# The first branch projection of a gated two-branch decoder block, computed in seven block products per pair of feature units (Strassen's scheme, one level)

## The chip, the cores and the metric

The kernel runs on one NeuronCore of a Trainium2 chip. The metric is device time in microseconds (us) for one launch. The kernel before was timed three times: 597.3, 597.81 and 597.81 us, median 597.81 us. One more execution was recorded by the profiler, and every duration in this text comes from that one.

The engines are named as in the profile: PE is TensorE (matmuls), PEld its weight loads, DVE is VectorE, ACT is ScalarE, POOL is GpSimd, SP is the queue that issues DMAs.

## The reference, cut to what matters

One decoder layer on 512 tokens and 16 meta tokens, width 1024, in float32. Two attention branches are computed from the same normed input `u`, each is gated, projected back to the model width, and the two are merged:

```python
u = rmsnorm(h, pre_norm_g)
proj = u @ w_in                       # all branch inputs and gates
...
o_mla = causal_block_attention(q_m, k_m, v_mla, MLA_SCALE)
y_mla = (o_mla * silu(z_mla)) @ w_br_mla            # 1024 x 1024, the second branch here (br 0)
...
o_fox = causal_block_attention(fq, fk, fv, FOX_SCALE, cum)
y_fox = (o_fox * silu(z_fox)) @ w_br_fox            # 1024 x 1024, the first branch here (br 1)
mixed = (sigmoid(gate_a) * y_mla + sigmoid(gate_b) * y_fox) @ w_out
h = h + rmsnorm(mixed, post_norm_g)
return h[:, N_META:]
```

The change is in the line for `y_fox` and in the order of the gate projections (`gate_a`, `gate_b`) around it.

## The kernel before

Every large matrix product is done in three passes. A float32 operand is split into a high part in the matmul type `fp32r` (an ACT copy) and the rest as a low part (a DVE or POOL subtraction), and the product is high x high + high x low + low x high. A weight that arrives by DMA as `wraw` (128 x 1024, 512 KB) so becomes `wh` and `wl`; the pool `wp` has three buffers of each of the three kinds, and a load waits until the buffer's earlier weight has been split.

Features lie on the partitions, in 8 blocks of 128 (`KD` = 8, `HK` = 4), tokens lie along the free dimension (`S` = 512). A "unit" (`unit`) is one output block of 128 features: 8 blocks of the contraction x 3 passes = 24 matmuls with a 128 x 128 weight held and 128 x 512 activations streamed, summed in one PSUM bank. A gate unit (`gate_unit`, tile `pg`) projects `u` and ends in a tanh on ACT into a tile `th` that a later step reads. A branch unit (`py`) projects the branch output `gT[br]` (split into `gh`, `gl` by `halved_g`) and ends in one DVE instruction, (th + 1) * PSUM, back into `gT[br]`.

The program has three stages: the input norm and small projections, sixteen attention stages (8 pairs of heads x 2 branches) with projections filled in between, and the merge stage. The change is in the merge stage. On PE the program order is kept as it is written (`manual_schedule`); ACT and DVE are ordered by a scheduler, each engine runs its own list in order, and SP issues the DMAs in its own order.

The merge stage before: `halved_g(1)` splits the first branch's output; then eight units `py(i, 1)`, with a gate unit after each of the first three; then `halved_g(0)` and four gate units; then eight units `py(i, 0)` of the second branch with the last four gate units between, and the sums for the output projection (`ssum`). The output projection itself is already done in seven block products on quarter matrices; the differences of its weight blocks (`tb`, loaded by eight DMAs in the merge stage) are formed by `tsum` on DVE.

The tanh results live in a pool `thp` of five buffers.

Of the kernel before, what the change touches and what calls it, by code (L numbers as in the profile page):

```python
# [11 lines left out]
F32 = mybir.dt.float32  # L12
F32R = mybir.dt.float32r
# [4 lines left out]
ALU = mybir.AluOpType  # L18
AX = mybir.AxisListType
PSUM = bass.MemoryType.PSUM  # L20
# [3 lines left out]
S = 512  # L24
META = 16
L = S + META
NH = 16
KD = D // 128
# [21 lines left out]
def f32(ap):  # L50
    return ap.bitcast(F32)
# [3 lines left out]
def block_kernel(ctx: ExitStack, tc: tile.TileContext, x, meta_tokens, pre_norm_g, w_in, fox_forget_b,  # L55
                 mla_q_norm_g, mla_kv_norm_g, w_uq, w_ukv, w_br_mla, w_br_fox, w_out, post_norm_g,
                 rope_tok, rope_pe, out):
    nc = tc.nc
# [4 lines left out]
    wbr = [w_br_mla[0].rearrange("(k p) f -> p k f", p=128), w_br_fox[0].rearrange("(k p) f -> p k f", p=128)]  # L63
# [19 lines left out]
    wp = ctx.enter_context(tc.tile_pool(name="wp", bufs=3))  # L83
    uid = [0]
# [3 lines left out]
    def dma(out, src, start=None):  # L88

        with tc.issue_after(sums_out[0]) if written[0] and sums_out else nullcontext():  # L90
            ins = (start or nc.sync.dma_start)(out=out, in_=src)
        if written[0]:
            tc.keep_in_program_order(ins)
        return ins.ins

    def mm(*a, **k):
        nc.tensor.matmul(*a, **k)  # L97
# [4 lines left out]
    def split_lo(eng, lo, src, hi):  # L102
        return eng.tensor_tensor(out=lo, in0=src, in1=f32(hi), op=ALU.subtract)  # L103
# [30 lines left out]
    def wunit(srcs):  # L134
        return wsplit(wload(srcs))
# [27 lines left out]
    thp = ctx.enter_context(tc.tile_pool(name="thp", bufs=5, side="right"))  # L163
# [9 lines left out]
    ths = {}  # L173
# [83 lines left out]
    with ExitStack() as ph:  # L257
# [262 lines left out]

    gctx = ctx.enter_context(ExitStack())
    PAIRED = [i + 4 * j for i in range(4) for j in range(2)]
    gates = [(i, 1) for i in range(KD)] + [(i, 0) for i in PAIRED]

    def gate_unit():

        i, br = gates.pop(0)

        def done(_, ps):
            ths[i, br] = thp.tile([128, L], F32, tag="th", name=f"th{i}{br}")[:, 0:S]  # L530
            nc.scalar.activation(ths[i, br], ps, AF.Tanh, scale=0.5)
        return unit(f"pg{i}{br}", win_w((O_GA, O_GB)[br], i), u_act, KD, REAL, done)


    with ExitStack() as att:
# [25 lines left out]
        gT = []  # L561
        masks, normed = [], []
# [361 lines left out]
        for si, (br, pr) in enumerate(stages):  # L924
            last = si + 1 == len(stages)
# [65 lines left out]
    with ExitStack() as mg:  # L991
        mg.enter_context(tc.manual_schedule(engines={mybir.EngineType.PE}))
        m1 = mg.enter_context(tc.tile_pool(name="m1", bufs=1, side="right"))
        mgg = ExitStack()
        m2 = mgg.enter_context(tc.tile_pool(name="m2", bufs=1))
        HK = KD // 2
        gh, gl = (m2.tile([128, KD, S], F32R, tag=n, name=n) for n in ("gh", "gl"))
        tb = [m1.tile([128, HK, 512], F32, tag=f"tb{n}", name=f"tb{n}") for n in range(4)]
        a1 = [m1.tile([128, HK, 256], F32R, tag=n, name=n) for n in ("a1h", "a1l")]
        a2 = [m1.tile([128, HK, S], F32R, tag=n, name=n) for n in ("a2h", "a2l")]  # L1000
        mx = gT[0]
        sh, sl = ([t.rearrange("p k s -> p (k s)")[:, 1024 * j : 1024 * j + 1024].rearrange("p (k s) -> p k s", k=HK)
                   for j in range(4)] for t in uT0)

        def halved_g(br):
            for k in range(KD):
                nc.scalar.copy(gh[:, k], gT[br][:, k])
                split_lo(nc.vector, gl[:, k], gT[br][:, k], gh[:, k])

        def py(i, br):  # L1010
            def get():
                return by_k(wunit([wbr[br][:, :, 128 * i : 128 * i + 128]])[0], KD)

            def done(_, ps):
                nc.vector.scalar_tensor_tensor(out=gT[br][:, i], in0=ths[i, br], scalar=1.0, in1=ps, op0=ALU.add, op1=ALU.mult)
            run(unit(f"py{i}{br}", get, lambda k: (gh[:, k, :], gl[:, k, :]), KD, [slice(0, S)], done))
            if br:
                return
            nc.vector.tensor_tensor(out=mx[:, i], in0=mx[:, i], in1=gT[1][:, i], op=ALU.add)
            src, (h, l) = (mx[:, i, 0:256], [t[:, i] for t in a1]) if i < HK else (mx[:, i], [t[:, i - HK] for t in a2])  # L1020
            nc.scalar.copy(h, src)
            split_lo(nc.vector, l, src, h)

        def tsum(n, half):

            ks = slice(2 * half, 2 * half + 2)
            t11, t12, t22, t21 = (t[:, ks] for t in tb)
            out, a, b = ((t11, t12, t11), (t12, t22, t12), (t22, t22, t11), (t21, t21, t22))[n]
            nc.vector.tensor_tensor(out=out, in0=a, in1=b, op=ALU.subtract)
# [9 lines left out]
                nc.scalar.copy(h[:, ks], x)  # L1039
                split_lo(nc.vector, l[:, ks], x, h[:, ks])  # L1040

        halved_g(1)
        for i in range(KD):
            py(i, 1)
            if i < 3:
                run(gate_unit())
            if i == 2:
                for n, (kb, c) in enumerate(((0, 0), (0, 1), (1, 1), (1, 0))):
                    for half in range(2):
                        k0 = HK * kb + 2 * half  # L1050
                        nc.sync.dma_start(tb[n][:, 2 * half : 2 * half + 2], wout[:, k0 : k0 + 2, 512 * c : 512 * c + 512])
            if i >= 4:
                for half in range(2):
                    tsum(i - 4, half)
# [72 lines left out]
        X, Z = ([op5.tile([128, 512], F32, tag="po", name=f"{n}{r}") for r in range(2)] for n in "xz")  # L1127
        Y = [acc(f"y{r}") for r in range(2)]
# [86 lines left out]
```

## Time and profile before

| | us |
|---|---|
| three timed runs | 597.3, 597.81, 597.81 |
| the profiled execution, time | 597.2 |
| the profiled execution, span from first to last instruction | 595.1 |
| PE busy | 586.8 (99%) |
| DVE busy | 379.2 (64%) |
| ACT busy | 343.1 (58%) |
| POOL busy | 201.6 (34%) |

The span is what the profile divides up; 2.1 us of the profiled execution's time lie outside it. A busy PE only says that some matmul was in flight: matmuls overlap, so a matmul's own duration is longer than the distance from its start to the next one's. What a row of matmuls costs is read from the chain of waits, which gives the stretch of time for a number of matmuls in a row. The mean granted TensorE clock was 0.997 of full.

### The profile page before, as it was taken

Reading aid. Unit: us, or ns where it says so; the run is one execution under the profiler, and the core shown is the slowest. Engines: PE = TensorE matmul, PEld = TensorE weight load, DVE = VectorE, ACT = ScalarE, POOL = GpSimd, SP = SyncE. Lnnn points to the kernel's source line nnn. Section 1 sums busy time; section 2 is a strip of 40 time slices with the busy share of each in tenths; the row PEclk is TensorE's granted clock in tenths of the full one; section 3 lists DMA queues with packets and bytes.
Section 4 is the critical chain, followed back from the end, with each engine's and each line's share of the span. In section 5 each row is a group of like instructions: output and inputs, shape, how many; then the busy total and the mean of one; then the engine's idle time right before and its main releaser. Section 6 shows DMA issues by size and latency. Waiting matters only on the chain.

```text
span 595.1 us, 10741 instructions
## 1 busy us (share of the span) xinstructions
PE 586.8 (99%) x3697; PEld 496.8 (83%) x3697; DVE 379.2 (64%) x1096; ACT 343.1 (58%) x785; POOL 201.6 (34%) x271
## 2 busy tenths in 40 slices
PE   8999999999999999999999999999999999999996
PEld 6989889889888888898898898878888888888884
DVE  5845876775776766757748747854634524377957
ACT  7846775784765765757748747942223422353753
POOL 4417656364458463544544554420000000000000
PEclk9999999999999999999999999999999999999998
DMA  8535699998995998896987887868533332333503
GB/s 298 118 82 172 124 165 269 217 206 202 181 198 125 208 225 219 187 184 166 201 166 175 190 171 149 193 165 305 155 85 92 106 107 73 105 106 104 215 2 141
DMA packets 219998, 97.45 MB, mean 164 GB/s; under 512 B 131456, under 2 KB 209672, under 8 KB 219944
## 3 DMA queue, kind: packets, MB, share of 16 engines
q1 hardware_dynamic: 219944, 96.77, 68.6%
q8 instruction: 29, 0.48, 0.3%
q14 instruction: 25, 0.20, 0.1%
HBM read 62.36 MB, written 3.97 MB: 111 GB/s over the span
## 4 chain that ended last, share of the span: by engine, by line
PE 98%; DMA 1%; SPq 0%; DVE 0%; issue 0%; POOL 0%; DVEq 0%; ACT 0%; POOLq 0%
PE z L97 17%; PE pg L97 15%; PE py L97 15%; PE v L97 9%; PE st L97 8%; PE fk L97 8%; PE fq L97 8%; PE ov L97 5%; PE psm L97 4%; PE x L97 4%; PE mq L97 2%; PE mk L97 1%; PE ppe L97 1%; PE y L97 1%; DMA wsr<-in_w_in_dram 1%; PE pt L100 1%
## 5 line engine op out<-in xcount | busy, mean ns | idle before, releaser
L103 POOL TENSOR_TENSOR wl<-wraw,wh 128x1024 fp32r<-128x1024 f32 (+2 forms) x62 | 119.6, 1936 | 92.5 <-ACT wh L130 70.1
L130 ACT CAST wh<-wraw 128x1024 fp32r<-128x1024 f32 (+1 forms) x80 | 83.1, 1042 | 116.0 <-PE pg L97 38.5
L787 ACT ACTIVATE sf<-sf,nb 128x272 f32<-128x272 f32 (+3 forms) x128 | 72.5, 568 | 16.8 <-DVE nb L779 15.3
L815 DVE SCALAR_TENSOR_TENSOR pn<-sf,ri,pn 128x128 f16<-128x128 f32 (+3 forms) x128 | 68.6, 576 | 6.6 <-ACT pn L814 6.2
L103 DVE TENSOR_TENSOR wl<-wraw,wh 128x1024 fp32r<-128x1024 f32 x34 | 41.5, 1222 | 42.1 <-ACT wh L130 42.0
L814 ACT ACTIVATE pn<-sf,ri 128x128 f16<-128x128 f32 (+3 forms) x128 | 61.2, 549 | 9.3 <-ACT sf L787 7.4
L97 PE MATMUL z<-uTh,wh 128*128 128x512 f32 x128 | 51.0, 398 | 0.0
L97 PE MATMUL pg<-uTh,wh 128*128 128x512 f32 x128 | 50.3, 393 | 0.0
L97 PE MATMUL z<-uTl,wh 128*128 128x512 f32 x128 | 50.2, 392 | 0.0
L97 PE MATMUL z<-uTh,wl 128*128 128x512 f32 x128 | 50.0, 390 | 0.0
L97 PE MATMUL pg<-uTh,wl 128*128 128x512 f32 x128 | 49.9, 389 | 0.0
L97 PE MATMUL pg<-uTl,wh 128*128 128x512 f32 x128 | 49.8, 389 | 0.0
L97 PE MATMUL py<-gh,wh 128*128 128x512 f32 x128 | 49.8, 389 | 0.0
L97 PE MATMUL py<-gl,wh 128*128 128x512 f32 x128 | 49.8, 389 | 0.0
L97 PE MATMUL py<-gh,wl 128*128 128x512 f32 x128 | 49.8, 389 | 0.0
L97 PE MATMUL st<-hlk,hlq 64*128 64x272 f32 (+3 forms) x480 | 45.5, 308 | 0.0
L97 PEld LDWEIGHTS st<-hlk,hlq 64*128 64x128 f32 x480 | 34.6, 185 | 6.0 <-ACT vh L702 2.8
L683 DVE TENSOR_REDUCE vsc<-v 128x1 f32<-128x272 f32 (+1 forms) x32 | 13.2, 432 | 39.9 <-PE v L97 39.9
L97 PE MATMUL v<-uTh,wl 128*128 128x256 f32 (+1 forms) x128 | 36.5, 285 | 0.0
L97 PE MATMUL fk<-uTl,wh 128*128 128x256 f32 (+1 forms) x128 | 36.5, 285 | 0.0
L97 PE MATMUL fk<-uTh,wh 128*128 128x256 f32 (+1 forms) x128 | 36.4, 285 | 0.0
L97 PE MATMUL v<-uTl,wh 128*128 128x256 f32 (+1 forms) x128 | 36.4, 285 | 0.0
(234 smaller groups left out, 1458.8 us busy)
## 6 DMA issues: line engine op xcount, KB each, us to landing
wraw<-in_w_in_dram SPq DMA_DIRECT2D x56, 512.0 KB, 4.6
cbp<-c_dram SPq DMA_DIRECT2D x16, 264.0 KB, 4.5
wraw<-in_w_br_fox_dram SPq DMA_DIRECT2D x8, 512.0 KB, 8.1
tb<-in_w_out_dram SPq DMA_DIRECT2D x8, 512.0 KB, 4.7
wraw<-in_w_br_mla_dram SPq DMA_DIRECT2D x8, 512.0 KB, 3.5
wraw<-in_w_out_dram SPq DMA_DIRECT2D x6, 512.0 KB, 3.7
xr<-in_x_dram SPq DMA_DIRECT2D x4, 512.0 KB
out_dram<-yo SPq DMA_DIRECT2D x8, 256.0 KB, 2.0
```

Of the source, the lines that this page charges most:

```text
L97: nc.tensor.matmul(*a, **k)
L100: nc.tensor.transpose(*a)
L103: return eng.tensor_tensor(out=lo, in0=src, in1=f32(hi), op=ALU.subtract)
L130: nc.scalar.copy(wh[:, :n], raw[:, :n])
L683: nc.vector.tensor_reduce(out=sc[:, i : i + 1], in_=ps, op=ALU.max, axis=AX.X, apply_absolute_value=True)
L787: exps[g] = nc.scalar.activation(sf, sf, AF.Exp, bias=sums["nb"][:, h, b : b + 1], scale=-1.0, accum_out=sums["su"][:, h, b : b + 1]).ins
L814: normed[:] = [nc.scalar.activation(hi, sf, AF.Copy, scale=rib).ins]
L815: nc.vector.scalar_tensor_tensor(out=lo, in0=sf, scalar=rib, in1=hi, op0=ALU.mult, op1=ALU.subtract)
```

## The change

The first branch's projection treats a pair of units (i, i + 4) at once. The weight's and the activations' halves (contraction blocks 0-3 and 4-7, tokens 0-255 and 256-511) make 2 x 2 block matrices, and the four output quarters come out of seven block products instead of eight. Each product is 4 contraction blocks x 3 passes = 12 matmuls with a 128 x 128 weight held and 128 x 256 activations streamed. The sums and differences that the scheme needs are formed on DVE: four of the activations once for all pairs, four of the weights in each pair. Every block that enters a product is split into a high and a low part (ACT copy, DVE subtraction): seven of the activations (128 x 1024 each) once, seven of the weights (128 x 512 each) in each pair.

Three PSUM banks a pair, X, Y and Z, hold the products. X runs through five of them: it is read by an ACT copy after the first and the third, by a DVE addition after the fifth, and at the end by the gating; each of the later products is added on top, so PE has to wait for that read before it starts the next product in X. The order on PE in a pair is X (A11), Z (S1), X (S2), Y (A12), X (S3), Z (S4), X (A22).

Two gate units run ahead of the first pair and two after each pair; one is left for the second branch's units. The gates are taken in the order 0, 4, 1, 5, ... for both branches, and two more tanh buffers (`thx`) are added.

```diff
-    gates = [(i, 1) for i in range(KD)] + [(i, 0) for i in PAIRED]
+    gates = [(i, br) for br in (1, 0) for i in PAIRED]
...
+        A11, A12, A22, S1 = ([t[:, kb[q], ts] for t in (gh, gl)] for q, ts in ((0, lo_), (1, lo_), (1, up), (0, up)))
+        S2, S3, S4 = a1, [t[:, :, lo_] for t in a2], [t[:, :, up] for t in a2]
...
+        def pair_py(i, br):
+
+            j, g, wb = i + HK, gT[br], wbr[br]
+            ra, rb = (wload([wb[:, :, 128 * f : 128 * f + 128]])[1] for f in (i, j))
+            yield
+            b11, b21, b12, b22 = ra[:, 0:512], ra[:, 512:], rb[:, 0:512], rb[:, 512:]
...
+            def prod(ps, a, w, first, last):
+                q = 0
+                for k in range(HK):
+                    for wx, ax in ((w[0], a[0]), (w[0], a[1]), (w[1], a[0])):
+                        mm(ps, wx[:, 128 * k : 128 * k + 128], ax[:, k], start=(first and q == 0), stop=(last and q == 11),
+                           skip_group_check=True)
+                        q += 1
+
+            def gated(dst, th, ts, ps, add):
+                if add:
+                    nc.vector.tensor_tensor(out=dst, in0=ps, in1=dst, op=ALU.add)
+                return nc.vector.scalar_tensor_tensor(out=dst, in0=th[:, ts], scalar=1.0, in1=dst if add else ps, op0=ALU.add, op1=ALU.mult)
+
+            w11 = take(b11)
+            comb(b11, b12, b11)
+            t1 = take(b11)
+            yield
+            comb(b12, b22, b12)
+            comb(b11, b22, b11)
+            t2 = take(b11)
+            prod(X, A11, w11, True, False)
+            nc.scalar.copy(c11, X)
+            w21 = take(b21)
+            prod(Z, S1, t1, True, False)
+            nc.scalar.copy(c22, Z)
+            t3 = take(b12)
+            comb(b21, b21, b11)
+            prod(X, S2, t2, False, False)
+            nc.scalar.copy(c12, X)
+            w22 = take(b22)
+            prod(Y, A12, w21, True, True)
+            gated(c11, th1, lo_, Y, True)
+            t4 = take(b21)
+            prod(X, S3, t3, False, False)
+            gated(c22, th2, up, X, True)
+            prod(Z, S4, w22, False, True)
+            gated(c12, th2, lo_, Z, True)
+            prod(X, A22, t4, False, True)
+            closed[i] = gated(c21, th1, up, X, False).ins
...
-        halved_g(1)
-        for i in range(KD):
-            py(i, 1)
-            if i < 3:
+        for i in range(HK):
+            for _ in pairs[i]:
+                pass
+            for half in range(2):
                 run(gate_unit())
...
         halved_g(0)
-        for _ in range(4):
-            run(gate_unit())
```

`take` gives a block of the weight its place in `wh` and `wl` and splits it there (`split_to`: an ACT copy, then a DVE subtraction); `comb` is one DVE addition or subtraction.

**DVE, the first branch's units, before.** One weight split (`wl`) and one gating instruction (L1015) for each unit; `gT_779` is the first branch's output, `wraw_5673` a gate's weight, the others are `py` weights:

```order
L103 TENSOR_TENSOR wl_5676<-wraw_5673,wh_5675 128x1024
L103 TENSOR_TENSOR wl_5717<-wraw_5714,wh_5716 128x1024
L1015 SCALAR_TENSOR_TENSOR gT_779<-th_5377,py_5647 128x512
L103 TENSOR_TENSOR wl_5749<-wraw_5746,wh_5748 128x1024
L103 TENSOR_TENSOR wl_5783<-wraw_5780,wh_5782 128x1024
L1015 SCALAR_TENSOR_TENSOR gT_779<-th_5408,py_5720 128x512
```

**DVE, the second pair's products, now.** `wl_5803` to `wl_5869` are the low parts of the pair's weight blocks t2, w21, t3, w22 and t4; `x_5790`, `y_5791` and `z_5792` are its PSUM banks; `wl_5916` and `wl_5949` belong to the two gate units behind the pair:

```order
L103 TENSOR_TENSOR wl_5803<-wraw_5786,wh_5802 128x512 x2
L1061 TENSOR_TENSOR wraw_5786<-wraw_5786 128x512
L103 TENSOR_TENSOR wl_5835<-wraw_5788,wh_5834 128x512 x2
L103 TENSOR_TENSOR wl_5869<-wraw_5786,wh_5868 128x512
L1093 TENSOR_TENSOR gT_779<-y_5791,gT_779 128x256
L1094 SCALAR_TENSOR_TENSOR gT_779<-th_5377,gT_779 128x256
L103 TENSOR_TENSOR wl_5916<-wraw_5913,wh_5915 128x1024
L1093 TENSOR_TENSOR gT_779<-x_5790,gT_779 128x256
L1094 SCALAR_TENSOR_TENSOR gT_779<-th_5408,gT_779 128x256
```

The low part of the next gate's weight, `wl_5916`, stands between the addition that reads Y and the one that reads X after the fifth product; PE's seventh product, which adds to X, has to wait for that second addition.

**ACT, the same places.** Before, the list held one cast for each unit's weight and a tanh (L531) for each gate unit:

```order
L130 CAST wh_5716<-wraw_5714 128x1024
L531 ACTIVATE th_5639<-pg_5614 128x512
L130 CAST wh_5748<-wraw_5746 128x1024
L130 CAST wh_5782<-wraw_5780 128x1024
L531 ACTIVATE th_5704<-pg_5679 128x512
```

Now, around the second pair's products, the casts of t3 and w22 (`wh_5834`) and the tanh of the gate unit ahead of the pair stand before the copies of X and Z (L1104, L1107, L1111); `wh_5915` is the cast of the next gate's weight:

```order
L1052 CAST wh_5834<-wraw_5788 128x512
L535 ACTIVATE th_5776<-pg_5751 128x512
L1052 CAST wh_5834<-wraw_5788 128x512
L1104 COPY gT_779<-x_5790 128x256
L1052 CAST wh_5868<-wraw_5786 128x512
L1107 COPY gT_779<-z_5792 128x256
L1111 COPY gT_779<-x_5790 128x256
L130 CAST wh_5915<-wraw_5913 128x1024
```

The copies that PE waits for are at fixed places in ACT's list: L1104 behind two weight casts and a tanh, the second copy of X (L1111) behind the cast of t4 and the copy of Z.

In the fourth pair the splits of the second branch's output (`gh`, from `gT_778`) stand among those copies as well:

```order
L1104 COPY gT_779<-x_6180 128x256
L1013 CAST gh<-gT_778 128x512 x2
L1052 CAST wh_6258<-wraw_6176 128x512
L1107 COPY gT_779<-z_6182 128x256
L1013 CAST gh<-gT_778 128x512 x2
L1111 COPY gT_779<-x_6180 128x256
L130 CAST wh_6305<-wraw_6303 128x1024
```

Four `gh` casts have come in ahead of the second copy of X, where the other pairs have none.

More of the change, by code (lines that the diff above doesn't have):

```diff
@@ L522, in block_kernel @@
     PAIRED = [i + 4 * j for i in range(4) for j in range(2)]
[L523 removed]
+    gates = [(i, br) for br in (1, 0) for i in PAIRED]
+    thx = [None]
     def gate_unit():
@@ L529, in done @@
         def done(_, ps):
-            ths[i, br] = thp.tile([128, L], F32, tag="th", name=f"th{i}{br}")[:, 0:S]
+            if len(ths) % 7 > 4:
+                ths[i, br] = thx[0].tile([128, S], F32, tag="thx", name=f"th{i}{br}")
+            else:
+                ths[i, br] = thp.tile([128, L], F32, tag="th", name=f"th{i}{br}")[:, 0:S]
             nc.scalar.activation(ths[i, br], ps, AF.Tanh, scale=0.5)
@@ new lines, in block_kernel, with comb, take @@
+        g11, g21, g12, g22 = (gT[1][:, kb[q], ts] for q, ts in ((0, lo_), (0, up), (1, lo_), (1, up)))
+        def comb(out, p, q, op=ALU.subtract):
+            nc.vector.tensor_tensor(out=out, in0=p, in1=q, op=op)
+        def pair_py(i, br):
[3 more added lines that the diff above has]
+            b11, b21, b12, b22 = ra[:, 0:512], ra[:, 512:], rb[:, 0:512], rb[:, 512:]
+            X, Y, Z = (sp.tile([128, 512], F32, tag="s", name=f"{n}{i}{br}")[:, 0:256] for n in "xyz")
+            c11, c21, c12, c22 = g[:, i, lo_], g[:, i, up], g[:, j, lo_], g[:, j, up]
+            th1, th2 = ths[i, br], ths[j, br]
+            room = []
+            def take(src):
+                if not room:
+                    uid[0] += 1
+                    hl = [wp.tile([128, 1024], F32R, tag=t, name=f"{t}{uid[0]}") for t in ("wh", "wl")]
+                    room.extend([[t[:, sl] for t in hl] for sl in (slice(0, 512), slice(512, 1024))])
+                to = room.pop(0)
+                split_to(to, src)
+                return to
+            def prod(ps, a, w, first, last):
[35 more added lines that the diff above has]
+            closed[i] = gated(c21, th1, up, X, False).ins
@@ new lines, in block_kernel @@
+        closed = {}
+        pairs = [pair_py(i, 1) for i in range(HK)]
+        with tc.issue_after(normed[0]):
+            split_to(A11, g11)
+            split_to(A22, g22)
+            comb(g22, g21, g22, ALU.add)
+            split_to(S1, g22)
+        run(gate_unit())
+        next(pairs[0])
+        with tc.issue_after(normed[0]):
+            comb(g21, g11, g21)
+            comb(g11, g22, g11)
+            split_to(S2, g11)
+        next(pairs[0])
+        run(gate_unit())
+        with tc.issue_after(normed[0]):
+            split_to(A12, g12)
+            comb(g12, g12, g11)
+            split_to(S3, g21)
+            split_to(S4, g12)
```

20 lines of the change are left out of this document (14 added, 6 removed).

## The prediction

> **What bounds the kernel now.** I read the page's first two parts, then the chain of waits in order of time, then the timeline of a few matmuls, then the groups.
>
> ```profile
> PE 586.8 (99%) x3697; PEld 496.8 (83%) x3697; DVE 379.2 (64%) x1096; ACT 343.1 (58%) x785; POOL 201.6 (34%) x271
> PE   8999999999999999999999999999999999999996
> 403.86:463.70 59.84, 59.84 (x266) 49.57 (x265) 30.60 (x32) 17.69 (x23) 0.00 (x0) 1.00 0.54 165
> ```
>
> PE is busy from start to end. The third row is the window of the first branch's units: PE 59.84 of 59.84 us, DVE 30.60, ACT 17.69, clock 1.00. So here a change pays what it takes from PE, less whatever time it makes PE wait. The chain of waits says what PE's work costs:
>
> ```profile
> 268.61 2.88 PE fk L97 x24
> ...
> 400.92 2.95 PE pg L97 x12
> 403.86 5.44 PE py L97 x24
> 409.30 5.44 PE pg L97 x24
> 414.74 5.44 PE py L97 x24
> ```
>
> A unit of 24 matmuls of 512 columns takes 5.44 us, 0.2267 us a matmul, with nothing between units although each waits for its weight. The second half of a key projection (`fk`) is 24 matmuls of 256 columns, the weight taken in the same pattern (high, high, low), 128 rows deep: 2.88 us, 0.120 us each. The groups seem to say something else:
>
> ```profile
> L97 PE MATMUL py<-gh,wh 128*128 128x512 f32 x128 | 49.8, 389 | 0.0
> L97 PE MATMUL fk<-uTh,wh 128*128 128x256 f32 x64 | 18.1, 283 | 0.0
> 268.45 0.28 PE L97 MATMUL fk<-uTh,wh 128*128 128x256 f32 x1
> 268.57 0.28 PE L97 MATMUL fk<-uTl,wh 128*128 128x256 f32 x1
> 268.69 0.28 PE L97 MATMUL fk<-uTh,wl 128*128 128x256 f32 x1
> ```
>
> 389 and 283 ns are from start to finish. The timeline shows starts 0.12 us apart with 0.28 us each: they overlap. With 283 ns the change would look 20 us dearer; the start distance is the price.
>
> **The matmuls.** Removed: eight units of the first branch, 8 x 5.44 = 43.52 us. Added: four pairs x seven products x 12 matmuls = 336 matmuls of 256 columns, 336 x 0.120 = 40.32 us. The sum on PE is -3.20 us. One eighth less multiplication gives only 7.4% less time, because two matmuls of 256 columns cost 0.240 us where one of 512 costs 0.2267. Gate units are moved, not added.
>
> The Trainium skill's Perfetto Trace Analysis, section Optimizing Tensor Performance, says that larger matmuls are more efficient than smaller ones; the rows agree, and put the loss at 5.9%. It speaks against the change without cancelling it.
>
> **What the other engines get.** Durations:
>
> ```profile
> L1007 ACT CAST gh<-gT 128x512 fp32r<-128x512 f32 x16 | 9.4, 617 | 0.3
> L531 ACT ACTIVATE th<-pg 128x512 f32<-128x512 f32 x16 | 9.4, 588 | 0.0
> L244 ACT CAST hlk<-fk 128x256 fp32r<-128x256 f32 x8 | 2.9, 369 | 4.0 <-PE fk L97 4.0
> L130 ACT CAST wh<-wraw 128x1024 fp32r<-128x1024 f32 x78 | 81.9, 1052 | 116.0 <-PE pg L97 38.5 <-issue 34.2 <-PE py L97 27.2
> L103 DVE TENSOR_TENSOR wl<-wraw,wh 128x1024 fp32r<-128x1024 f32 x34 | 41.5, 1222 | 42.1 <-ACT wh L130 42.0
> L1019 DVE TENSOR_TENSOR gT<-gT,gT 128x512 f32<-128x512 f32 x8 | 5.5, 691 | 0.2
> L1037 DVE TENSOR_TENSOR gT<-gT 128x256 f32<-128x256 f32 x8 | 3.4, 421 | 0.1
> L1029 DVE TENSOR_TENSOR tb<-tb,tb 128x1024 f32<-128x1024 f32 x8 | 9.6, 1221 | 4.6 <-DMA tb<-in_w_out_dram 4.4
> ```
>
> A pair and its two gate units are 28 x 12 / 4 = 84 matmuls and 48: 10.08 + 10.88 = 20.96 us of PE. DVE gets in that time seven weight subtractions and four sums (11 x 0.69 = 7.6), seven output instructions of 256 columns (three sums at 0.42; the four gatings are not in the trace at this width, and stand between 0.42 and the 0.69 of 512 columns; I take 0.42: 2.9 in all), two gate splits (2.4) and two to four `tb` subtractions (2.4 to 4.9): 15.3 to 17.8 us. ACT gets 7 x 0.62 + 3 x 0.37 + 2 x (1.05 + 0.59) = 8.7 us. Both fit, so the only question is whether one comes late at a given place.
>
> **The three hand-backs of X** are the part that the trace of before does not show. Count from a pair's first matmul; product n starts at (n - 1) x 1.44 us. Each hand-back is a wait that was not there before; behind PE's waiting matmul stands all the rest of the program.
>
> Product 3 waits for ACT's first copy of X. ACT's list ahead of it: the cast of t3 (its buffer comes free when the gate unit ahead ends, at 0), the tanh, the cast of w22, the copy: 0.62 + 0.59 + 0.62 + 0.37 = 2.20, against 2.88. Slack 0.68.
>
> Product 5 waits for the second copy: product 3 ends at 4.32, copy to 4.69, against 5.76. In the fourth pair four `gh` casts stand ahead: 2.20 + 4 x 0.62 + 0.62 (t4) + 0.37 (Z) + 0.37 = 6.04 against 5.76, 0.28 late if every duration counts in full.
>
> Product 7 waits for DVE's addition of X, with the next gate's low part ahead of it. That gate's cast waits for the buffer that product 4 reads, until 5.76: cast to 6.81, subtraction to 8.03, addition to 8.45, against 8.64. Slack 0.19, the smallest of all.
>
> ```profile
> 388.69 1.65 ACT L1007 CAST gh<-gT 128x512 fp32r<-128x512 f32 x3
> 418.31 3.49 DVE L1029 TENSOR_TENSOR tb<-tb,tb 128x1024 f32<-128x1024 f32 x3
> L97 PEld LDWEIGHTS py<-gh,wl 128*128 128x128 f32 x64 | 12.0, 188 | 2.5
> ```
>
> Two things stand around these sums. Back to back, three casts take 1.65 us (0.55 each) and three subtractions 3.49 (1.16), so the lists are a little faster. And a weight load of 0.19 us goes ahead of a matmul; if the wait holds it back too, 0.19 us of slack is gone. Bounds: from no stall to 3 x 0.2 + 0.3 = 0.9 us. I take 0.2, near the lower end, because the back-to-back rows give about what the weight load takes.
>
> **Before the first pair.** The splits of the activations are 7 x 1.22 + 4 x 1.22 = 13.4 us of DVE, and they stand behind the last attention norm.
>
> ```profile
> 386.78 1.46 DVE L815 SCALAR_TENSOR_TENSOR pn<-sf,ri,pn 128x512 f16<-128x512 f32 x2
> 400.96 0.75 DVE L833 SCALAR_TENSOR_TENSOR gT<-ov,vsc,sil 128x512 f32<-128x512 f32 x1 [2.56 <-PE ov L97]
> ```
>
> From 388.2 to the first pair at 403.86 + 10.88 = 414.74 there are 26.5 us. DVE needs 13.4 + two gate splits 2.4 + the last `gT` 0.75 + five steps of the first weights 3.5 = 20.1. The cover is the two gate units put ahead (10.88 us); without them DVE would end 20.1 - 15.6 = 4.5 us after the pair's start, and PE would wait for up to that. With them I cost it at nothing.
>
> **The loads.** Their number is the same; each waits for a buffer's split, in SP's order.
>
> ```profile
> wraw<-in_w_in_dram SPq DMA_DIRECT2D x56, 512.0 KB, 4.6
> wraw<-in_w_br_fox_dram SPq DMA_DIRECT2D x8, 512.0 KB, 8.1
> 401.74 1.71 SPq L1051 DMA_DIRECT2D tb<-in_w_out_dram  x3
> 406.06 0.37 SPq L91 DMA_DIRECT2D wraw<-in_w_in_dram  x1
> 406.47 4.51 SPq L1051 DMA_DIRECT2D tb<-in_w_out_dram  x5
> ```
>
> The weight of the gate unit behind a pair goes out once the second gate unit ahead of that pair has been split. That gate's cast waits for product 6 of the pair before (8.64), then 1.05 + 1.22 and an output instruction or two: about 11 of 20.96 us, 10 before the next pair. Landing in 8.1 us at worst it is there 2 us before the pair, and needed 5.76 after its start. A pair's second weight goes out after the first gate's split (8.03), is there at 16.1 and needed at about 20.4. The eight `tb` loads keep their place on SP, three ahead of a gate's weight (406.06 here) and five behind it; that weight is needed 5.76 us into the first pair, at 420.5. Cost 0, with 4 us and more of cover everywhere; a load later than that costs what it is later.
>
> **After the fourth pair** two gate units cover the rest of `halved_g(0)`, where four did. DVE after product 7 (10.08): 0.42 + four `tb` 4.9 + four `gl` 2.8 + a weight 1.2 ends at 19.4; the second branch starts at 20.96. Cost 0, slack 1.6; beyond it each us of DVE is one of PE.
>
> **The small edits.** The gates' order and the two tanh buffers: a tanh behind a pair needs a buffer that the pair's gatings give back, the last about 0.5 us after the pair's end, and is itself due 5.44 us after it. Cost 0.
>
> **The sum.** -3.20 + 0.2 = -3.0 us. The profiled execution of before took 597.2 us (span 595.1 and 2.1 around it), which gives 594.2; the median of the timed runs lies 0.6 higher, which gives 594.8. I forecast 594.5 us, between them; with the bounds of the stalls and of the base, 593.9 to 595.7. A measurement of this kernel can tell about 0.2%, 1.2 us, from no change.
>
> **Rivals.** All count from 597.5, the middle of the two bases.
>
> *Slower: the seventh product waits behind the gate's weight.* The addition of X is held by the gate's subtraction, that by its cast, that by its load. Whatever the load, ACT or DVE is late beyond the 0.19 us is lost in each of four pairs; it outweighs the gain from 0.8 us a pair. At 2 us a pair: 597.5 - 3.2 + 8.0 = 602.3. For it: the place in the list and the small slack. Against it: the load's cover of over 7 us, and a window where DVE is half idle. Chance 0.13. The Trainium skill's Perfetto Trace Analysis, section Optimizing Tensor Performance, asks that independent matmul groups rotate through different PSUM banks so that emptying one overlaps the next group; X here is emptied under a single product. No row of before shows a bank taken back so soon.
>
> *Most of the gain is eaten.* Every hand-back costs 0.15 us (12 x 0.15 = 1.8, for instance the weight load held back each time): 597.5 - 3.2 + 1.8 = 596.1. Chance 0.12, with about 0.05 of it within 0.2%.
>
> *More gain.* The other half of a key projection has 272 columns:
>
> ```profile
> 259.82 2.96 PE fk L97 x24
> ```
>
> 24 matmuls of 272 columns in 2.96 us are 0.1233 each; the line through 272 and 512 columns gives 0.1164 at 256, not 0.120. If the merge stage reaches it, 336 x 0.1164 = 39.1, a gain of 4.4: 593.1. Against it: all 256-column groups of the trace stand at 0.120. Chance 0.05. The Trainium skill's TensorE: Matmul & The Clock Gate, section Back-to-back issue gap, has N / 2.4 GHz + 2.5 ns for isolated matmuls (109 ns at 256 columns); by it the gain would be 4.8 us, an estimate; the trace's 120 ns decides.
>
> That the change doesn't do what it says is excluded by the built order, which holds 336 matmuls of 256 columns in place of 192.
>
> **How the numbers follow.** Forecast case 0.70, more gain 0.05, eaten 0.12, slower 0.13. Faster by over 0.2%: 0.70 + 0.05 + 0.07 = 0.82; within: 0.05; slower: 0.13. The range runs from the larger gain, 593.1, to the eaten case with the upper base and stalls, 596.8.
>
> **What would show it.** Right: the chain of waits has `x`, `z`, `y` pieces of 12 matmuls at 1.44 us, 84 in 10.08 us, PE idle near 0 between 414 and 500, and the second branch's first unit about 3 us earlier against the gates done. Wrong: PE idle before `x` with DVE `gT` L1093 (the seventh product) or ACT `gT` L1104/L1111 (third, fifth) as releaser, or 12 matmuls that take more than 1.44 us.

## The result and the profile after

| | before | after |
|---|---|---|
| median of the timed runs | 597.81 us (597.27 to 598.5, 6 runs) | 594.53 us (594.06 to 594.73, 6 runs) |
| profiled execution, its span | 597.2, 595.1 | 594.59, 592.5 |
| granted clock | 0.997 | 0.998 |

The changed kernel takes 0.9944 of the time before, with a 95% interval of 0.9934 to 0.9955 (so are the intervals of ratios below). 594.5 us was forecast.

The page's first part, of after:

```profile
PE 584.1 (99%) x3841; PEld 501.0 (85%) x3841; DVE 412.3 (70%) x1155; ACT 357.8 (60%) x816; POOL 200.3 (34%) x271
```

The window from the first pair's start to the fourth's end (busy us of PE, its weight loads, DVE, ACT and POOL, then clock, DMA share and GB/s):

```profile
415.56:488.32 72.76, 72.76 (x481) 66.70 (x481) 50.55 (x79) 32.66 (x57) 0.00 (x0) 1.00 0.45 126
```

The view of waits, all rows of PE (us in total, times, longest):

```profile
PE spun L97 <- DVE KPL L231: 1.5, 1, 1.5
PE psm L97 <- POOL wsh L298: 1.1, 1, 1.1
```

PE is busy from end to end, as before, though DVE now works 50.55 of the window's 72.76 us. Both waits lie ahead of the first branch's stage. That PE waits nowhere in it is still not the whole truth, as the pieces of a pair show. The chain of waits of after (start, length, what); the second pair is the seven pieces of 12 matmuls:

```profile
399.76 1.97 PE ov L97 x26
401.73 13.83 PE pg L97 x60
...
436.49 1.43 PE x L97 x12
437.92 1.44 PE z L97 x12
439.36 1.38 PE x L97 x12
440.74 1.42 PE y L97 x12
442.16 1.38 PE x L97 x12
443.54 1.36 PE z L97 x12
444.90 1.61 PE x L97 x12
446.52 10.91 PE pg L97 x48
...
499.22 5.44 PE py L97 x24
...
548.18 5.49 PE x L97 x24
```

The two ends of the stage in the chain of before:

```profile
398.95 1.97 PE ov L97 x26
...
550.74 5.49 PE x L97 x24
```

From the last attention output (`ov`) to the first unit of the output projection went 550.74 - 398.95 = 151.79 us, and now 548.18 - 399.76 = 148.42: 3.37 less. The time at which the stage begins differs by up to 1.1 us from one profile to the next (398.95 here, 400.08 in run 11); the length of the stage leaves that out, so it is the measure used for the experiments. Two things in the pair were not forecast: the products are not all 1.44 (the third, fifth and sixth take 1.36 to 1.38, the fourth 1.42), and the seventh takes 1.61.

### The profile page after: what moved, and what is told of

The parts are those of the page before. It is cut to its first block, busy times and chain, and to the rows that moved or that the text cites. A ratio compares the mean times of both kernels' runs of the same rounds, so it can differ in the third digit from the quotient of the medians.

```text
span 592.5 us, 11129 instructions
## 1 busy us (share of the span) xinstructions
PE 584.1 (99%) x3841; PEld 501.0 (85%) x3841; DVE 412.3 (70%) x1155; ACT 357.8 (60%) x816; POOL 200.3 (34%) x271
## 4 chain that ended last, share of the span: by engine, by line
PE 97%; DMA 1%; SPq 0%; DVE 0%; issue 0%; POOL 0%; DVEq 0%; ACT 0%; POOLq 0%
PE z L97 19%; PE pg L97 15%; PE v L97 9%; PE st L97 8%; PE fk L97 8%; PE fq L97 8%; PE x L97 8%; PE py L97 7%; PE ov L97 5%; PE psm L97 4%; PE y L97 2%; PE mq L97 2%; PE mk L97 1%; DMA wsr<-in_w_in_dram 1%; PE ppe L97 1%; PE pt L100 1%
## 5 line engine op out<-in xcount | busy, mean ns | idle before, releaser
L130 ACT CAST wh<-wraw 128x1024 fp32r<-128x1024 f32 (+1 forms) x72 | 74.6, 1040 | 53.5 <-PE py L97 16.8
L103 DVE TENSOR_TENSOR wl<-wraw,wh 128x512 fp32r<-128x512 f32 (+1 forms) x54 | 51.0, 947 | 27.5 <-ACT wh L1052 18.9
L1052 ACT CAST wh<-wraw 128x512 fp32r<-128x512 f32 x28 | 17.3, 619 | 39.8 <-DVE wraw L1061 15.4
L97 PE MATMUL fk<-uTh,wl 128*128 128x256 f32 (+1 forms) x128 | 36.4, 285 | 0.0
L97 PE MATMUL v<-uTh,wh 128*128 128x256 f32 (+1 forms) x128 | 36.4, 285 | 0.0
```

The costliest lines, as they stand in the source:

```text
L130: nc.scalar.copy(wh[:, :n], raw[:, :n])
L1052: nc.scalar.copy(to[0], src)
```

## Experiments

**1. The addition ahead of the gate's low split.** Why is the seventh product longer? The timeline of after at the change from the sixth product (`z`) to the seventh (`x<-gh`), rows of DVE, of the weight loads (PEld) and of the matmuls:

```profile
443.21 1.23 DVE L103 TENSOR_TENSOR wl<-wraw,wh 128x1024 fp32r<-128x1024 f32 x1
444.35 0.42 DVE L1093 TENSOR_TENSOR gT<-x,gT 128x256 f32<-128x256 f32 x1
...
444.52 0.19 PEld L97 LDWEIGHTS z<-a2h,wl 128*128 128x128 f32 x1
444.82 0.19 PEld L97 LDWEIGHTS x<-gh,wh 128*128 128x128 f32 x1
...
444.63 0.28 PE L97 MATMUL z<-a2h,wl 128*128 128x256 f32 x1
444.82 0.39 PE L97 MATMUL x<-gh,wh 128*128 128x256 f32 x1
```

The weight load of a matmul usually starts 0.11 us ahead of it and 0.11 after the load before. Here it comes 0.30 after the load before, at 444.82, just behind the end of the addition that empties X (444.35 + 0.42 = 444.77). So the wait seems to hold back the load as well, and the delay is 0.19 us. It isn't in the view of waits, since the matmul before is still shown busy until 444.91.

```diff
+ xadd, adds = [], {}        # the DVE addition of X of the pair just written
...
- split_lo(low[0], wl[:, :n], raw[:, :n], wh[:, :n])
+ with tc.issue_after(xadd[0]) if xadd else nullcontext():
+     split_lo(low[0], wl[:, :n], raw[:, :n], wh[:, :n])
```

> The changed kernel with one order turned round on DVE: behind each pair, the addition that empties X for the seventh product stands ahead of the low split of the next gate's weights instead of behind it. Theory (the seventh product waits for that addition): it starts as soon as the sixth is through, its 12 matmuls take 1.42 us as the other products with gh and gl do instead of 1.61 (1.58 in the third and fourth pair), and the kernel is 4 x 0.17 = 0.7 us faster, 593.8; the gate behind then begins 0.17 earlier, and its low split, 0.42 later than now, is wanted only when the seventh product is through, so the gate should not wait. Rival (the seventh product is dear in itself, by its operands or by the place in the pair): 1.6 stays, and the time is 594.5.

Measured: 593.66 us (593.43 to 594.04), ratio to before 0.9928 (0.9916 to 0.9941). The stage takes 147.71, 0.71 less than after. In its timeline the addition stands ahead of the split, and the load comes on time:

```profile
443.22 0.42 DVE L1095 TENSOR_TENSOR gT<-x,gT 128x256 f32<-128x256 f32 x1 [0.57 <-PE x L97]
443.57 1.22 DVE L103 TENSOR_TENSOR wl<-wraw,wh 128x1024 fp32r<-128x1024 f32 x1
...
444.20 0.19 PEld L97 LDWEIGHTS x<-gh,wh 128*128 128x128 f32 x1
```

The seventh product in its chain of waits:

```profile
444.48 1.42 PE x L97 x12
```

The stall theory holds, with its size; the next gates don't wait (10.91, as in after). This version is the fastest of the study along with number 11, which differs from it only in the place of two buffers that PE doesn't read.

**2. The addition 0.42 us later.**

```diff
  prod(X, S3, t3, False, False)
- gated(c22, th2, up, X, True)
+ again = nc.vector.tensor_tensor(out=b12[:, 0:256], in0=X, in1=c22, op=ALU.add).ins
+ with tc.issue_after(again):
+     gated(c22, th2, up, X, True)
```

> The changed kernel with one more DVE addition of 256 columns (0.42 us; it writes into a buffer that nobody reads) between the gate's low split and the addition that empties X, in each of the four pairs. Theory (the seventh product already waits for this addition): each pair grows by the whole 0.42, the seventh product from 1.6 to 2.0, and the kernel by 4 x 0.42 = 1.7 us, 596.2. Rival (there is still slack, and 1.6 is the product's own pace): less than half of that, under 595.3.

Measured: 596.44 us (595.97 to 597.29). The stage takes 150.25, 1.83 more than after, 0.46 a pair: the 0.42 and the gap between two instructions. Now the wait is long enough to be seen in the view of waits:

```profile
PE x L97 <- DVE gT L1093: 1.4, 4, 0.4
```

And in the timeline, the load and the first matmul of the second pair's seventh product:

```profile
445.47 0.19 PEld L97 LDWEIGHTS x<-gh,wh 128*128 128x128 f32 x1 [0.58 <-DVE gT L1093]
...
445.48 0.38 PE L97 MATMUL x<-gh,wh 128*128 128x256 f32 x1 [0.38 <-DVE gT L1093]
```

Of a delay of about 0.65 us (0.19 and 0.46) the matmul's row shows 0.38, the load's row 0.58. The load is the row to read. There is no slack left at this place in the changed kernel: the added time was lost in full.

**3. The gates moved alone.**

```diff
- gates = [(i, 1) for i in range(KD)] + [(i, 0) for i in PAIRED]
+ gates = [(i, br) for br in (1, 0) for i in PAIRED]
...
+ for _ in range(2):
+     run(gate_unit())
- for i in range(KD):
+ for i in range(HK):
      py(i, 1)
+     py(i + HK, 1)
+     for _ in range(2):
+         run(gate_unit())
```

> The kernel before, with the gate units alone put where the changed kernel has them (two ahead, two behind each two projection units, in its order, with its two more buffers for their results), and the projection units as they were. Theory (TensorE runs through, and gates cost 10.88 a pair wherever they stand): no change, 597.8 within 0.3. Rival (the new order gains or loses by itself): a difference over 0.5 either way, which would have to be taken out of what the seven products bring.

Measured: 597.9 us (597.58 to 598.23), ratio 1.0001 (0.9992 to 1.0011). The stage takes 151.79, as before. The order of the gates by itself brings nothing and costs nothing, and the 3.37 us belong to the seven products.

**4. Two halves of 256 columns, no seven products.**

```diff
+ sls = [slice(0, 256), slice(256, 512)] if br else [slice(0, S)]
- run(unit(f"py{i}{br}", get, lambda k: (gh[:, k, :], gl[:, k, :]), KD, [slice(0, S)], done))
+ run(unit(f"py{i}{br}", get, lambda k: (gh[:, k, :], gl[:, k, :]), KD, sls, done))
```

> The kernel before, with each of the eight projection units of the first branch done in two halves of 256 columns, one after the other with the weights loaded again: 8 x 48 matmuls of 256 columns for 8 x 24 of 512, no scheme of seven products. It measures the price of the smaller shape by itself. By the products with gh and gl of the changed kernel (0.119 us a matmul): 48 x 0.119 = 5.71 a unit for 5.44, 8 x 0.27 = 2.2 us more, 600.0. By those with a1 and a2 (0.1135): 5.45, no change, 597.8. If halving a matmul's columns halved its time: no change either.

Measured: 600.27 us (599.98 to 600.63), ratio 1.0044 (1.0029 to 1.0059); the stage takes 154.43, 2.64 more. The chain of waits shows a unit of 48 matmuls:

```profile
415.88 5.75 PE py L97 x48
```

That is 0.120 us a matmul, the price that the prediction took from `fk`. Halving the columns costs 5.75 / 5.44 = 5.7% here. Seven eighths of 8 x 5.75 = 46.0 are 40.25, so at this price the change would bring 3.27 before any stall. But in the changed kernel three products are cheaper than this, which is the question of the other runs.

**5. gh, gl and the sums of g exchanged.** In the built program gh and gl start at 90,880 and 107,264 bytes of each partition, a1 and a2 from 161,216 on.

```diff
- m1 = mg.enter_context(tc.tile_pool(name="m1", bufs=1, side="right"))
+ m1 = mg.enter_context(tc.tile_pool(name="m1", bufs=1))
- m2 = mgg.enter_context(tc.tile_pool(name="m2", bufs=1))
+ m2 = mgg.enter_context(tc.tile_pool(name="m2", bufs=1, side="right"))
```

> The changed kernel with two groups of buffers exchanged in SBUF: the high and low parts of g (gh, gl), now at 91 to 124 KB of each partition, go to 153 to 186 KB, and the sums of g (tb, a1, a2) go where these were; the instructions and their order stay. Theory of the place (a product reads its moving operand at a pace that hangs on where in SBUF it lies): the products with gh and gl (A11, S1, A12, A22), now 1.42 to 1.44 us, fall to 1.36 to 1.38, and those with a1 and a2 (S2, S3, S4) rise to 1.42; four of seven instead of three are cheap, 4 x 0.06 = 0.24 us off, and units of 512 columns in the second branch, 5.44, could fall as well: 594.3 or, with these, up to 2 us less. Rival, theory of the moment (the pace hangs on what DVE and ACT do at that time of the pair): the seven durations stay as they are, and the time is 594.5.

Measured: 595.18 us (595.02 to 595.69). The chain of waits: the third product of the first pair; of the fourth pair the first product (gh), the third (a1), the fourth (gh) and the sixth (a2); the second branch's first unit.

```profile
417.88 1.63 PE x L97 x12
...
477.76 1.41 PE x L97 x12
...
480.59 1.43 PE x L97 x12
482.02 1.38 PE y L97 x12
...
484.82 1.44 PE z L97 x12
...
498.57 5.60 PE py L97 x24
```

The moment is out: the pace goes with the buffers. The products with gh and gl fell and those with a1 and a2 rose. But the units of 512 columns rose too, 5.60 for 5.44, which the theory of the place had the other way. And the run was not as clean as its expectation says: in their new place the sums were split later, so that on ACT a cast of `a2h` stood ahead of the first copy of X in the first pair, and the third product waited there (1.63). The timeline of ACT:

```profile
416.43 1.05 ACT L1052 CAST a2h<-gT 128x1024 fp32r<-128x1024 f32 x1
417.38 0.37 ACT L1104 COPY gT<-x 128x256 f32<-128x256 f32 x1
```

**6. Both edits**, the addition first (1) and the exchange (5).

> Both edits of the two runs before this one: X is emptied ahead of the gate's low split, and gh and gl change places with tb, a1 and a2. If the two theories hold, the gains add: 0.7 and 0.24 or more, 593.6 or less. If only the stall is real, 593.8; if neither is, 594.5.

Measured: 594.95 us (594.72 to 595.09). The gains did not add: the exchange lost 1.3 us on the first (units of 5.60), and the addition first won only 0.24 of stage (149.33 for 149.57), since with dearer products ahead of it (2.86 for the fifth and sixth together, 2.74 in after) the seventh had little to wait for.

**7 and 8. A hole ahead of gh**, of 704 and of 64 bytes, in the kernel with the addition first.

```diff
+ m2.tile([128, 176], F32, tag="gap", name="gap")    # 16 instead of 176 in the second
  gh, gl = (m2.tile([128, KD, S], F32R, tag=n, name=n) for n in ("gh", "gl"))
```

> The kernel with the addition first (593.66 us), and a hole of 704 bytes ahead of gh, so that gh and gl (and nothing else that TensorE reads) start 704 bytes higher in each partition: at 91,584 instead of 90,880. Counted modulo 2048 bytes this is 1472, where a1 and a2 start; the sums stay where they are. Theory of the start (the pace of 256 columns hangs on where a row of the moving operand starts within a block of bytes): the products with gh and gl fall from 1.42 to 1.44 us to 1.36 to 1.38, 16 x 0.06 = 1.0 us in all, while the units of 512 columns in the second branch rise from 5.44 to 5.60, as they did when gh and gl were at 153,024, also 1472 modulo 2048, 8 x 0.16 = 1.3 us; sum +0.3, 594.0. Rival (the pace hangs on the region of SBUF, near the weights or far): nothing changes, 593.7.

> As the run before, with a hole of 64 bytes: gh and gl start at 90,944, 832 modulo 2048. Theory of the start: the pace of the products with gh and gl and of the units of 512 columns changes by some hundredths of a microsecond a product, to a side that nothing shows yet. Rival, theory of the region: products 1.42 to 1.44, units 5.44, 593.7.

Measured: 595.2 us (594.98 to 595.62) and 594.53 (594.15 to 594.85); stages 149.15 and 148.52. With 704 bytes, the chain of waits has, of the second pair's first product (gh) and third (a1), of the second branch and of the output projection:

```profile
435.98 1.41 PE x L97 x12
...
438.80 1.41 PE x L97 x12
...
498.30 5.60 PE py L97 x24
...
548.56 5.60 PE x L97 x24
```

The theory of the region falls: gh is in the same region and PE's pace changed. But the theory of the start had it only half right. Units of 512 columns went to 5.60 as forecast; the products with gh and gl fell to 1.41, not 1.38, and those with a1 and a2, which were not moved, rose to 1.41. With 64 bytes all seven are at 1.41 or 1.42 and second-branch units at 38.47 / 7 = 5.50.

**9. The sums 704 bytes lower**, gh in its old place; the hole stands behind `a2`.

```diff
  a2 = [m1.tile([128, HK, S], F32R, tag=n, name=n) for n in ("a2h", "a2l")]
+ m1.tile([128, 176], F32, tag="gap", name="gap")
```

> The kernel with the addition first (593.66 us), with the sums tb, a1 and a2 704 bytes lower (a1 at 160,512 instead of 161,216, which is 768 modulo 2048, as gh is), while gh, gl and all else stay. With the hole of 704 bytes ahead of gh both had 1472 and all seven products took 1.41. Theory of the difference (the pace hangs on whether successive moving operands start at the same place modulo 2048): all seven products become alike, at about 1.41, and the units of 512 columns stay at 5.44, so 28 x 1.41 = 39.5 for 39.3 now, 593.9. Rival (the place of gh alone sets the state of the whole stage): products as now, 1.43, 1.44, 1.38, 1.42, 1.38, 1.36, 1.42, and 593.7.

Measured: 594.47 us (594.23 to 595.0); the stage takes 148.68. All seven products became alike, as the theory of the difference had it, but at 1.44 and not at 1.41. The chain of waits, the second pair's first product (gh) and third (a1):

```profile
436.08 1.43 PE x L97 x12
...
438.96 1.44 PE x L97 x12
```

**10. The weights 704 bytes higher**, and with them gh and gl. In the merge stage it differs from number 7 in the place of the weight buffers alone; in the stages ahead other buffers move with them.

```diff
+ ctx.enter_context(tc.tile_pool(name="gapp", bufs=1)).tile([128, 176], F32, tag="gap", name="gap")
  wp = ctx.enter_context(tc.tile_pool(name="wp", bufs=3))
```

> The kernel with the addition first, with a hole of 704 bytes ahead of the weight buffers: the weights (raw, high and low parts) and gh and gl move up by 704 and start, like a1 and a2, at 1472 modulo 2048; u's parts uTh and uTl, the moving operand of the gate units, stay at 768. Two kernels had one place for all moving operands and weights at 768: moving operands at 768 gave 1.44 a product and 5.44 a unit of 512 columns, at 1472 they gave 1.41 and 5.60. Theory A (what counts is the start of the moving operand against that of the weights): products 1.44 and second-branch units 5.44 again, while the gate units, now with different starts, go from 5.44 to 5.60 in the last stage (16 of them, 2.6 us) and the units of 512 columns of u in the stages ahead may change too; 596 or more. Theory B (the moving operand's own start counts): products 1.41, second-branch units 5.60, gates 5.44, as with the hole ahead of gh: 595.2.

Measured: 596.77 us (596.74 to 598.23), ratio to before 0.9992 (0.9982 to 1.0002). The chain of waits: the two halves of a key projection in an attention stage (272 and 256 columns), the second pair's third product, the gates behind it, the second branch's first unit, and two units of the output projection, the first with a1 as weights, the second with u:

```profile
260.42 3.04 PE fk L98 x24
...
269.32 2.82 PE fk L98 x24
...
439.88 1.44 PE x L98 x12
...
447.08 11.20 PE pg L98 x48
...
500.84 5.48 PE py L98 x24
...
549.96 5.44 PE x L98 x24
...
566.43 5.60 PE x L98 x24
```

Theory A holds. The operands are where they were in number 7, yet products are back at 1.44 and second-branch units near 5.44 (38.13 for the last seven, 5.45 each), because the weights moved along; the gates, whose operand u stayed behind, went to 11.00 for the two behind the first pair and 11.20 for the others. What counts is where the moving operand starts against the weights, not where it starts by itself. The stage takes 149.95, 2.24 more than in number 1, and the whole kernel 3.11 more; within the noise, the hole takes the change's gain away.

**11. The hole behind gl**, so that only two buffers of gate results move.

```diff
+ m2.tile([128, 176], F32, tag="gap", name="gap")
  thx[0] = mgg.enter_context(tc.tile_pool(name="thx", bufs=2))
```

> The kernel with the addition first, with the hole of 704 bytes behind gl instead of ahead of gh: of the buffers that the hole moved in the earlier run only the two small ones of gate results (read by DVE, never by TensorE) still move. Theory (what TensorE reads sets its pace): nothing changes, products 1.42 to 1.44 and 1.36 to 1.38, units 5.44, 593.7. Rival (the accesses of DVE and ACT to these two buffers did it): all products 1.41 and units 5.60, 595.2.

Measured: 593.57 us (593.1 to 596.34); the stage takes 147.72, as with the addition first alone (147.71), and every piece is as there. The buffers of DVE and ACT are out.

**12. The sums 448 bytes lower**, as number 9 with 112 in place of 176.

> The kernel with the addition first, with the sums tb, a1 and a2 448 bytes lower: a1 and a2 start 256 bytes past the weights' and gh's start, counted modulo 512 (the step from one block of weights to the next), where they were 192 past it, and 0 with the sums 704 lower. If the pace goes by a start modulo 256 or less, 256 is like 0: all seven products 1.44, 594.5. If it goes by the whole distance within 512, the products differ again, some of 1.36 to 1.42 as now, or to another pace that no run has shown; with all as now, 593.7.

Measured: 594.73 us (594.39 to 595.0), and the stage 148.68, to the hundredth that of number 9, with 1.43 and 1.44 for all products. A distance of 256 bytes does the same as none.

The six arrangements side by side, with the distance from the weights' start to the moving operand's, modulo 256 bytes (addresses of the built program), and pieces of the chain in us, those with a wait left out:

| kernel | gh, gl | a1, a2 | u | products with gh | with a1, a2 | 512 columns of gh | two gates |
|---|---|---|---|---|---|---|---|
| after, 1, 11 | 0 | 192 | 0 | 1.42 to 1.44 | 1.36 to 1.38 | 5.44 | 10.91 |
| 9, 12 | 0 | 0 | 0 | 1.43, 1.44 | 1.44 | 5.44 | 10.91 |
| 10 | 0 | 0 | 64 | 1.43, 1.44 | 1.44 | 5.45, the first 5.48 | 11.00, 11.20 |
| 7 | 192 | 192 | 0 | 1.41 | 1.41 | 5.60 | 10.88 |
| 8 | 64 | 192 | 0 | 1.41, 1.42 | 1.41 | 5.50 | 10.92 |
| 5, 6 | 192 | 0 | 0 | 1.38 to 1.41 | 1.42 to 1.44 | 5.60 | 10.89 |

## Why the prediction was right

The mechanism is the forecast one: PE runs through, and the sum of its pieces sets the time. But two terms were mis-sized, and their errors partly cancelled. That 594.53 meets 594.5 so closely is luck: from the median of 597.81 the kernel gained 3.28, 0.28 more than the forecast 3.0, and the base that the forecast counted from, 597.5, lies 0.31 below that median. Summed over the stage, in us:

| step | forecast | measured | from |
|---|---|---|---|
| eight units removed | -43.52 | -43.52 | 3: four times 10.88, stage unchanged |
| 336 matmuls added | +40.32 | +39.33 | 1: pairs of 9.83, without the stall |
| hand-backs of X | +0.2 | +0.72 | pairs of 40.05 in all in after, 39.33 in 1 |
| gates moved | 0 | +0.12 | pairs of gates at 10.91 for 10.88 |
| sum | -3.0 | -3.35 | the stage: -3.37 |

**The price of a matmul.** The start distance was the right thing to read: 0.120 us is what 256 columns cost here, by run 4 and by runs 9, 10 and 12, not the 0.283 of the groups. But it isn't one number. The products with a1 and a2 ran at 0.113 to 0.115 us, with buffers 192 bytes off the weights' start, between products at distance 0; with both at 192 (run 7) it is 0.1178. The mean of the 336 is 39.33 / 336 = 0.117, near the 0.1164 of the line through 272 and 512 columns, but run 9 shows that this was the accident of an address: with the sums lower all 336 are at 0.120.

The line itself mixed two places, which no row of before shows apart. By the kernel's slices the 272 columns begin 64 bytes ahead of the tokens that the gates read, so 192 off the weights modulo 256, and the 256 columns behind them at 0. Run 10 moves them to 0 and 64 (and other buffers of that stage as well): the pieces of 2.96 and 2.88 become 3.04 and 2.82. With 3.04 / 24 = 0.1267 for 272 columns the line gives 0.120 at 256.

**The hand-backs.** The third and the fifth product never waited, as forecast. The timeline of ACT has both copies of the second pair, and the second of the fourth, which was feared 0.28 late:

```profile
437.96 0.37 ACT L1104 COPY gT<-x 128x256 f32<-128x256 f32 x1
...
440.78 0.37 ACT L1111 COPY gT<-x 128x256 f32<-128x256 f32 x1 [0.56 <-PE x L97]
...
483.03 0.37 ACT L1111 COPY gT<-x 128x256 f32<-128x256 f32 x1
```

They end at 438.33, 441.15 and 483.40; the products start at 439.36, 442.16 and 484.00. The seventh did wait, 0.16 to 0.19 us in each pair. The step that failed is the slack of 0.19: the prediction set the weight load of 0.19 us against the faster lists and called it even. The timeline of after has the first matmul of the second pair:

```profile
436.33 0.28 PE L97 MATMUL x<-gh,wh 128*128 128x256 f32 x1
```

Counted from it, the addition ends at 444.77 - 436.33 = 8.44, where 8.45 was forecast: the lists in sum were no faster. But the six products ahead take 8.41 instead of 8.64, and the seventh's load was due 0.11 ahead of its matmul, at 444.63, or 8.30. So 0.19 of slack became 0.14 too late, and the gain in the price made the stall: in run 5, where the fifth and sixth product take 2.86 together and not 2.74, the seventh takes 1.42 to 1.47 for the 1.38 of run 6, a wait of 0.04 to 0.09. The prediction's own sign of being wrong, 12 matmuls that take more than 1.44 us, was there in each pair; the cost of 0.72 for the forecast 0.2 is the term that it had too small. It lies within the stated bounds of 0 to 0.9.

**The rivals.** The slower one was right in mechanism and place: the seventh product does wait behind the next gate's low split, and by run 2 what comes on top is lost in full. It stayed small: in the second pair that gate's cast starts at 442.12, as soon as the fourth product's end at 442.16 allows (its modelled end; the cast's row names that product as releaser), so no load held it up. The Trainium skill's Perfetto Trace Analysis, section Optimizing Tensor Performance, asks that independent matmul groups rotate through different PSUM banks, so that emptying one overlaps the next group. X's products are added onto one another in one bank and so are not independent as they stand; taking the bank back cost 0.72 us here, and run 1 saves it by an order alone, with the same banks. Of the other two, 0.15 us at every hand-back did not come (4 of 12 waited). The larger gain's price came nearly (39.33 for 39.1), and the stall took 0.72 of the 0.99 that it won. The upper end of the range, 596.8, is 0.4 more than its case adds up to (597.8 - 3.2 + 1.8 = 596.4); nothing hangs on it here.

**Cover.** Nothing ahead of the first pair, no load and nothing behind the fourth pair cost PE time. DVE's last rows ahead of the second branch in the timeline of after:

```profile
493.75 2.49 DVE L103 TENSOR_TENSOR gl<-gT,gh 128x512 fp32r<-128x512 f32 x4
496.16 2.35 DVE L103 TENSOR_TENSOR wl<-wraw,wh 128x1024 fp32r<-128x1024 f32 x2
```

All is done at 498.51, and the unit starts at 499.22 right behind the gates. One weight was forecast in this stretch and there are two; the unit needs only its own. That one was loaded first (its DMA goes out at 482.73, the next gate's at 486.25), so it is very likely the first of the two rows, done near 497.4. The unit's first weight load starts at 498.84, so about 1.4 was left of a forecast slack of 1.6.

## What to carry to other kernels

Price a change of shape by the distance between starts, and where a PSUM buffer is taken back within a group of products, count the release against the weight load of the waiting matmul, not against the matmul: a stall of 0.2 us did not show in the view of waits here, but it did in the lengths of equal pieces. An order that empties the buffer first, ahead of work that isn't wanted yet, can save time at no cost (0.7 us here). And where a pool's size or side changes, look at where TensorE's operands now start against its weights before explaining a difference of half a per cent by the edit.

## What was not expected of the hardware

At a granted clock of 0.997 to 0.999 the pace of TensorE went with the distance between the starts of the moving operand and the weights in a partition. The distances are given modulo 256 bytes, because run 12 has 256 more than run 9 and the same stage to the hundredth; no other pair of distances 256 apart was compared. For 512 columns (24 matmuls) distance 0 gave 5.44 us, 64 bytes 5.50 in run 8 and 5.60 a gate unit in run 10, 192 bytes 5.60. The first two units of the output projection show the same in before: 5.49 with a1 as weights, which becomes 5.44 with the sums lower (runs 9 and 12). For 256 columns (12 matmuls) it is the other way: distance 0 throughout gave 1.44, 192 throughout 1.41, and a mix of the two as little as 1.36. Moving buffers by 704 bytes changed the kernel by up to 3.1 us (593.66 to 596.77), nearly as much as the whole change brought. The Trainium skill's SBUF — State Buffer, section A bandwidth-pool intuition that's wrong (but worth ruling out), gives TensorE a second, independent read port for weight loads. It says nothing there of start addresses; that the two starts count against each other all the same is what these runs show, and they do not show why.

Three things stay open. Why a mix of two distances runs faster than either alone. Why the same distance of 64 bytes gave 5.50 and 5.60: counted modulo 512 the two are 64 and 320, but even in run 10 alone, with the same operands, a gate unit took 5.50 behind the first pair and 5.60 behind the others, and in run 7 the output projection's first units kept the 5.60 of the units before them. So the distance alone does not set the pace, and what ran before may play a part. And whether other distances give the better pace for both shapes, which was not tried.
